# The first mixer's norm by another road: turned on VectorE and ScalarE between interleaved units, with the entrance norm's weights put in front of x and tile 0 fetched first

## The chip, the core and the metric

The kernel runs on one core of a Trainium2 chip. Its engines work side by side, each through its own list of instructions in order: TensorE (PE) multiplies matrices into PSUM, VectorE (DVE) and ScalarE (ACT) do elementwise work, GpSimd (POOL) does little here, and SyncE (SP) issues DMA transfers, which 16 DMA engines carry. They wait for each other by semaphores. The metric is device time in microseconds (us) from the kernel's start to its end; lower is better.

## The reference, cut to what matters

Two layers on x of 256 tokens by 1024 channels. The change touches the first half of layer 0, a gated short convolution:

```python
def rms_norm(x, g):
    y = x * lax.rsqrt(jnp.mean(x * x, axis=-1, keepdims=True) + EPS)
    return y * g

def short_conv_mixer(h, w_in, conv_w, w_out):
    b_gate, c_gate, hx = jnp.split(h @ w_in, 3, axis=-1)
    return (b_gate * causal_dwconv(c_gate * hx, conv_w)) @ w_out

x = x + short_conv_mixer(rms_norm(x, a_norm), a_w_in, a_conv, a_w_out)
x = x + conv_glu_ffn(rms_norm(x, f_norm[0]), ...)
# then shared K/V, attention, a second conv_glu_ffn, a last rms_norm
```

All is float32.

## The kernel before

x stands transposed in SBUF, channels on partitions, as 8 tiles k of [128 channels, 256 tokens]. Weights come in *units*: B units of 1 MB (128 x 2048) and S units of 0.5 MB (128 x 1024). To keep float32's accuracy with fast matmuls, each operand is split into a high and a low half: `hi(tag)` makes ACT write the high half of the next unit of that size (a rounding copy), `lo(tag)` makes DVE write the low half (raw minus high) of the next one; both may do a part, as in `hi("B", 0, 4)`, the first quarter. After the last part of a low half, the raw buffer is free and SP issues the load of the unit three further on. `hi` does nothing if the unit whose high buffer it would overwrite has not been given to TensorE yet. A product is three matmuls (`mm3`): high weight by high x, high weight by low x, low weight by high x.

The mixer has eight units of channels j. MC[j] (B) gives c_gate and hx, MB[j] (S) gives b_gate, MO[j] (S) is the row block of the output matrix. B units come in the order MC[0] to MC[7], then the FFN's; S units MB0, MB1, MB2, MB3, MO0, MO1, MB4, MO2, MB5, MO3 and so on. TensorE's order is MC0 and MB0 (in four quarters along k, as x and weights land), MC1, MB1, MC2, MB2, MC3, MB3, MO0, MO1, MC4, MB4, MO2, MC5 ...

The norm's weight is applied to x before the split (`scaled_hi`, `scaled_lo`), the per-token factor (the row rr, and its square in `rr[:, 1, :]`) after the matmuls: `mixer_a(j)` forms u = c * rr^2 * hx on DVE (two products), starts the convolution cv on ACT, does two taps and a product on DVE; `mixer_b(j)` multiplies by b_gate and splits the result z[j], high half on ACT and low half on DVE. So no unit can leave PSUM before rr is known, while units 0 to 2 are multiplied without it. In PSUM there are three `up` banks, four `acc` banks and one `misc`.

Here rr comes from `rstd_cols` and `rstd_rows`: TensorE sums the squares over partitions into columns (line 371), DVE takes the root, makes diagonal matrices dh and dl of it (lines 382, 383), and TensorE spreads them to all partitions by a matmul with ones (`each`, line 390). The FFN and attention norms use `sums`, `roots`, `spread` and `rows`: a transpose on DVE in 32 x 32 blocks, a reduction, three small ACT copies that bring four groups of 32 partitions together, a second reduction, the root (a first guess and three rounds of three instructions) on 32 partitions, three copies back, and a transpose that broadcasts.

At the start ten matmuls on `ones` (line 142) keep TensorE at work until data lands. `pk` holds all norm weights and convolution weights; its first 72 columns come over ACT's queue. `xh.again` and `xl.again` are copies of x tile 0 at another address; `up_step(..., again=True)` reads them instead of tile 0. The order of all this is written out by hand; no scheduler moves it.

Of the kernel before, what the change touches and what calls it, by code (L numbers as in the profile page):

```python
# [11 lines left out]
F32 = mybir.dt.float32  # L12
# [25 lines left out]
def f32(ap):  # L38
    return ap.bitcast(F32)
# [3 lines left out]
def yoco_kernel(ctx: ExitStack, tc: tile.TileContext, t: dict, out: bass.AP):  # L43
# [18 lines left out]
    class Unit:  # L62
# [12 lines left out]

        def load(self, part=0, parts=1):
# [3 lines left out]
            nc.sync.dma_start(self.raw[:, c], self.src[:, c])  # L80

# [55 lines left out]
    ones = const.tile([128, 128], F32, name="ones")  # L137
    G.memset(ones, 1.0)
    each = const.tile([128, 192], F32R, name="each")[:, 48:176]
    warm = psum.tile([128, 512], F32, name="misc", bufs=1)  # L140
    for _ in range(10):
        PE.matmul(warm[:, :128], ones, ones, start=True, stop=True)  # L142
# [21 lines left out]
    def par(c, k=0):  # L164
        return pk[:, c + k:c + k + 1]

# [66 lines left out]
    def acc_bank():  # L233
        return psum.tile([128, 2, S], F32, name="acc", bufs=4)
# [108 lines left out]

    def roots(sq):

        t = sq[0:32, 4, :]
        w = tmp.tile([128, 8], F32, name="nw")
        ms = t[:, 32:40]
        V.tensor_reduce(ms, t[:, 0:32].rearrange("p (a b) -> p b a", a=4), axis=mybir.AxisListType.X, op=OP.add)
# [17 lines left out]
    def rstd_cols(sq, meanwhile=None):

        ps = psum.tile([128, 512], F32, name="misc", bufs=1)
        for c in range(2):  # L370
            PE.matmul(ps[:, c:c + 1], sq[:, 2, c * 128:(c + 1) * 128], ones[:, 0:1],
                      start=(c == 0), stop=True, skip_group_check=True)
        w = tmp.tile([128, 8], F32, name="nw")
        ms, y, a = w[:, 0:2], w[:, 2:4], w[:, 4:6]
        V.tensor_scalar(ms, ps[:, 0:2], 1.0 / D, EPS, op0=OP.mult, op1=OP.add)
        rsqrt(ms, y, a)
        if meanwhile:
            meanwhile()
        dh, dl = (tmp.tile([128, 384 + 64], F32R, name="d" + x, tag="z" + x, bufs=4)[:, 16:16 + S] for x in "hl")
        for c in range(2):  # L380
            d = slice(c * 128, c * 128 + 128)
            V.tensor_scalar(dh[:, d], ident, y[:, c:c + 1], None, op0=OP.mult)
            V.scalar_tensor_tensor(dl[:, d], ident, y[:, c:c + 1], f32(dh[:, d]), op0=OP.mult, op1=OP.subtract)
        return y, (dh, dl)

    def rstd_rows(dg, scales=(1.0,), orders=(same,)):

        ps = psum.tile([128, 512], F32, name="misc", bufs=1)
        for n in range(2):
            PE.matmul(ps[:, :S], each, dg[n], start=(n == 0), stop=(n == 1), skip_group_check=True)  # L390
        r = act.tile([128, 2, S], F32, name="rr", bufs=1)
        for n, s in enumerate(scales):
            A.activation(r[:, n, :], orders[n](ps[:, :S]), AF.Copy, scale=s)
        return r

# [83 lines left out]
    rr = None  # L479

    def mixer_a(j, fill=None):

        w = [par(P_CONV, 3 * j + n) for n in range(3)]
        m = tmp.tile([128, 2, S], F32, name="u", bufs=2)
        V.tensor_mul(m[:, 1, :], mc[j][:, 0, :], rr[:, 1, :])
        V.tensor_mul(m[:, 0, :], mc[j][:, 1, :], m[:, 1, :])
        o = tmp.tile([128, 2, S], F32, name="cv", bufs=2)
        A.activation(o[:, 0, :], m[:, 0, :], AF.Identity, scale=w[2])
        hi("B")
        if fill:  # L490
            lo(fill)
        tap(o[:, 0, :], m[:, 0, :], w[1], 1)
        tap(o[:, 0, :], m[:, 0, :], w[0], 2)
        V.tensor_mul(o[:, 1, :], o[:, 0, :], rr[:, 0, :])
        return o[:, 1, :]

    def mixer_b(j, o, fill=None):
        hid = tmp.tile([128, S], F32, name="hid", tag="sc", bufs=4)
        V.tensor_mul(hid, mb[j][:, 0, :], o)
        z[j], zh, zl = split_act(hid, S)  # L500
        zh()
        if fill:
            lo(fill)
        zl()

    mc[1] = acc_bank()
    up_step(MC[1], mc[1], xh, xl, 2, range(1, 8), first=1)
    MC[1].used = False

    def quarter(q):  # L510
        hi("B", q, 4)
        lo("B", q, 4)

    _, dg = rstd_cols(sq, lambda: quarter(0))
    for q in range(1, 4):
        quarter(q)
    hi("S")
    hi("B")
    up_step(MC[1], mc[1], xh, xl, 2, (0,), first=1, again=True)
    MC[1].used = True  # L520
    mb[1] = acc_bank()
    up_step(MB[1], mb[1], xh, xl, 1, (*range(1, 7), 0, 7), first=1)
    mc[2] = up_bank()
    up_step(MC[2], mc[2], xh, xl, 2, range(0, 2))
    rr = rstd_rows(dg)
    A.activation(rr[:, 1, :], rr[:, 0, :], AF.Square)
    lo("S")
    up_step(MC[2], mc[2], xh, xl, 2, range(2, 8))
    mb[2] = psum.tile([128, 512], F32, name="misc", bufs=1).rearrange("p (a s) -> p a s", s=S)
    up_step(MB[2], mb[2], xh, xl, 1)  # L530
    for i in range(2):
        o = mixer_a(i, "B")
        hi("S")
        mixer_b(i, o, "S")
    hi("S")
    mc[3] = up_bank()
    up_step(MC[3], mc[3], xh, xl, 2, (1, 2, 3, 4, 5, 6, 0, 7), first=1, again=True)
    mixer_b(2, mixer_a(2, "S"))
# [34 lines left out]
    def ffn(layer, xh, xl, sq, bank=down_bank, between=None):  # L573
# [468 lines left out]
def _lay_out(i):  # L1042
# [41 lines left out]
```

## Time and profile before

| | before |
|---|---|
| runs shown | 564.45, 565.1 and 804.78 us, median 565.1 |
| profiled execution | 564.47 us |
| its span, first to last instruction | 562.7 us |
| TensorE busy | 556.1 us (99%) |
| DVE busy | 473.5 us (84%) |
| ACT busy | 343.7 us (61%) |
| read from HBM | 106.65 MB, 191 GB/s over the span |

In the rows of the profile below, a row in order of time gives the start in us, the time that it took in us (of several merged instructions: from the first's start to the last's end), the engine, the line, the operation, output<-inputs by the program's names, the shapes, how many (x), and in brackets how long the engine was idle before and what ended that. Rows with one duration as min/median/max are groups of equal instructions, in ns. Matmuls are pipelined: one is listed with 0.28 us but the next starts 0.11 us after it.

### The profile page before, as it was taken

How to read it: one execution, taken by the hardware profiler on the slowest of the kernel's cores; microseconds unless marked ns; L12 is line 12 of the kernel's file. 1: busy time of each engine (PE TensorE's matmuls, PEld its weight loads, DVE VectorE, ACT ScalarE, POOL GpSimd, SP SyncE). 2: the span in 40 equal slices, each digit the busy share in tenths (PEclk: the TensorE clock that was granted, in tenths of full speed). 3: DMA queues.
4: the chain of work that ended last, by engine and by line, in shares of the span. 5: the costliest groups of instructions: out<-in, count | busy, mean ns of one | idle time of the engine just before them, and what ended most of it. 6: DMA issues, size and time to landing. Idle time of an engine off the chain costs nothing.

```text
span 562.7 us, 11827 instructions
## 1 busy us (share of the span) xinstructions
PE 556.1 (99%) x4890; PEld 552.4 (98%) x4890; DVE 473.5 (84%) x827; ACT 343.7 (61%) x541; POOL 9.6 (2%) x29
## 2 busy tenths in 40 slices
PE   9999999999999999999999999999999999999996
PEld 9999999999999999999999999999999999999995
DVE  6998869998877787787997999859999888889875
ACT  7765437756654565465767777657676456546444
POOL 0400000000000000000000000000000000000001
PEclk9999999999999999999999999999999999999998
DMA  8986583447446545645354566552656654563211
GB/s 293 389 303 226 191 295 119 167 155 263 174 181 225 194 160 209 225 171 204 112 193 158 201 211 216 193 220 86 246 194 225 225 195 162 206 223 114 76 39 75
DMA packets 24181, 108.48 MB, mean 193 GB/s; under 512 B 2736, under 2 KB 5440, under 8 KB 16192
## 3 DMA queue, kind: packets, MB, share of 16 engines
q1 hardware_dynamic: 23840, 107.43, 53.7%
q8 instruction: 38, 0.62, 0.4%
q10 hardware_dynamic: 288, 0.30, 0.2%
q14 instruction: 15, 0.12, 0.1%
HBM read 106.65 MB, written 1.07 MB: 191 GB/s over the span
## 4 chain that ended last, share of the span: by engine, by line
PE 98%; issue 0%; ACT 0%; POOL 0%; DVE 0%; POOLq 0%
PE up L169 20%; PE up L171 20%; PE up L170 19%; PE acc L169 7%; PE acc L171 7%; PE acc L170 7%; PE acc L200 3%; PE acc L202 3%; PE acc L203 3%; PE up L442 1%; PE up L817 1%; PE acc L687 1%; PE acc L690 1%; PE acc L689 1%; PE misc L142 1%; PE acc L742 1%
## 5 line engine op out<-in xcount | busy, mean ns | idle before, releaser
L169 PE MATMUL up<-xh,hiB 128*128 128x256 f32 x928 | 256.5, 276 | 0.0
L171 PE MATMUL up<-xh,loB 128*128 128x256 f32 x928 | 256.2, 276 | 0.0
L170 PE MATMUL up<-xl,hiB 128*128 128x256 f32 x928 | 256.2, 276 | 0.0
L169 PEld LDWEIGHTS up<-xh,hiB 128*128 128x128 f32 x928 | 174.2, 188 | 0.5 <-issue 0.3
L170 PEld LDWEIGHTS up<-xl,hiB 128*128 128x128 f32 x928 | 174.2, 188 | 0.0
L171 PEld LDWEIGHTS up<-xh,loB 128*128 128x128 f32 x928 | 174.2, 188 | 0.0
L97 DVE TENSOR_TENSOR loB<-rawB,hiB 128x2048 fp32r<-128x2048 f32 (+3 forms) x80 | 148.2, 1856 | 3.7 <-ACT hiB L91 3.6
L91 ACT ACTIVATE hiB<-rawB 128x2048 fp32r<-128x2048 f32 (+2 forms) x75 | 123.8, 1657 | 11.7 <-PE up L170 4.3
L588 ACT ACTIVATE cv<-u,pk 128x256 f32<-128x256 f32 x88 | 48.2, 595 | 69.6 <-DVE u L581 69.4
L97 DVE TENSOR_TENSOR loS<-rawS,hiS 128x1024 fp32r<-128x1024 f32 (+2 forms) x73 | 83.5, 1146 | 6.8 <-ACT hiS L91 6.8
L426 DVE SCALAR_TENSOR_TENSOR cv<-u,pk,cv 128x255 f32<-128x255 f32 x192 | 81.3, 478 | 2.7 <-ACT cv L588 1.7
L91 ACT ACTIVATE hiS<-rawS 128x1024 fp32r<-128x1024 f32 (+2 forms) x73 | 72.0, 987 | 9.4 <-PE acc L170 5.2
L171 PE MATMUL acc<-sh,loS 128*128 128x256 f32 x240 | 66.2, 276 | 0.0
L169 PE MATMUL acc<-sh,hiS 128*128 128x256 f32 x240 | 66.2, 276 | 0.0
L170 PE MATMUL acc<-sl,hiS 128*128 128x256 f32 x240 | 66.2, 276 | 0.0
L581 DVE TENSOR_TENSOR u<-up,rr 128x512 f32<-128x512 f32 x44 | 30.3, 688 | 42.6 <-PE up L171 42.2
L423 ACT ACTIVATE sh<-hid 128x256 fp32r<-128x256 f32 x52 | 21.7, 417 | 58.4 <-DVE hid L605 53.7
L169 PEld LDWEIGHTS acc<-sh,hiS 128*128 128x128 f32 x240 | 45.1, 188 | 0.0
L170 PEld LDWEIGHTS acc<-sl,hiS 128*128 128x128 f32 x240 | 45.1, 188 | 0.0
L171 PEld LDWEIGHTS acc<-sh,loS 128*128 128x128 f32 x240 | 45.0, 188 | 0.0
L200 PE MATMUL acc<-hiS,sh 128*128 128x256 f32 x154 | 42.5, 276 | 0.0
L202 PE MATMUL acc<-loS,sh 128*128 128x256 f32 x154 | 42.5, 276 | 0.0
(209 smaller groups left out, 791.1 us busy)
## 6 DMA issues: line engine op xcount, KB each, us to landing
rawB<-w_up SPq DMA_DIRECT2D x44, 1024.0 KB, 4.7
rawS<-w_dn SPq DMA_DIRECT2D x44, 512.0 KB, 3.4
rawB<-w_qk SPq DMA_DIRECT2D x8, 1024.0 KB, 4.7
rawB<-w_mc SPq DMA_DIRECT2D x6, 1024.0 KB, 8.0
rawS<-w_mo SPq DMA_DIRECT2D x8, 512.0 KB, 5.4
rawB<-w_v SPq DMA_DIRECT2D x4, 1024.0 KB, 4.8
rawS<-w_o SPq DMA_DIRECT2D x8, 512.0 KB, 4.4
rawS<-w_mb SPq DMA_DIRECT2D x7, 512.0 KB, 5.8
```

Of the source, the lines that this page charges most:

```text
L91: A.activation(self.hi[:, c], self.raw[:, c], AF.Copy)
L97: V.tensor_sub(self.lo[:, c], self.raw[:, c], f32(self.hi[:, c]))
L169: PE.matmul(o, wh, xh, start=start, stop=False, skip_group_check=True)
L170: PE.matmul(o, wh, xl, start=False, stop=False, skip_group_check=True)
L171: PE.matmul(o, wl, xh, start=False, stop=stop, skip_group_check=True)
L200: PE.matmul(o, hh[:, tok], u.hi[:, f], start=(first and (apart or d.start == 0)), stop=False, skip_group_check=True)
L202: PE.matmul(o, hh[:, tok], u.lo[:, f], start=False, stop=False, skip_group_check=True)
L203: PE.matmul(o, hl[:, tok], u.hi[:, f], start=False, stop=last, skip_group_check=True)
L423: return (h, lw), lambda: A.activation(h, src, AF.Copy), lambda: V.tensor_sub(lw, src, f32(h))
L426: V.scalar_tensor_tensor(o[:, back:], u[:, :S - back], w, o[:, back:], op0=OP.mult, op1=OP.add)
L581: V.tensor_mul(u, ub[j], rr[:, 0:1, :].to_broadcast([128, 2, S]))
L588: A.activation(o[:, half, :], u[:, half, :], AF.Identity, scale=cw[half][2], bias=par(P_FCB, c0 + half * FJ))
```

## The change

Four things are changed together. (1) At the entrance, the eight weights of the first norm and 56 columns of padding stand in front of x in one array; tile 0 with them is the first transfer, tile 1 the second, MC[0]'s first eighth is issued by ACT, and tile 0 and its weights are split before tile 1 is touched. DVE instead of POOL writes `ones`, and seven warm-up matmuls run instead of ten. `pk` comes in one transfer, later. (2) rr comes by `sums`, `roots`, `spread`, `rows`, with quarters of MC[2]'s splits between their steps; `rstd_cols` and `rstd_rows` go, and the copy of xl's tile 0 moves from DVE to ACT. (3) `mixer_a` and `mixer_b` are cut into `mixer_u`, `mixer_t`, `mixer_z` and a separate low half, and for units 0 to 3 these are interleaved with each other and with the splits in a new order. MC[1] is multiplied in one go, tile 0 as copy and seventh. (4) The FFN's third unit in layer 0 reads a copy of tile 0, which ACT makes after the first.

```diff
     ones = const.tile([128, 128], F32, name="ones")
-    G.memset(ones, 1.0)
-    each = const.tile([128, 192], F32R, name="each")[:, 48:176]
+    V.memset(ones, 1.0)
+    spare = const.tile([128, 192], F32, name="each")
-    for _ in range(10):
+    for _ in range(7):
         PE.matmul(warm[:, :128], ones, ones, start=True, stop=True)
+    MC[0].load(0, 8, nc.scalar)
-    A.activation(each, ones, AF.Copy)
-    xT = act.tile([128, KT, S], F32, name="xres", bufs=1)
-    nc.scalar.dma_start(pk[:, :P_FCW], t["pk"][:, :P_FCW])
-    for q in range(4):
-        nc.sync.dma_start(xT[:, 2 * q:2 * q + 2, :], t["xT"][:, 2 * q:2 * q + 2, :])
+    xg = act.tile([128, 64 + KT * S], F32, name="xres", bufs=1)
+    xT = xg[:, 64:].rearrange("p (k s) -> p k s", s=S)
+    for a, b in ((0, 64 + S), (64 + S, 64 + 2 * S)):
+        nc.sync.dma_start(xg[:, a:b], t["xT"][:, a:b])
+    MC[0].load(1, 8)
+    MB[0].load(0, 4)
+    for q in range(1, 4):
+        a = 64 + 2 * q * S
+        nc.sync.dma_start(xg[:, a:a + 2 * S], t["xT"][:, a:a + 2 * S])
         MC[0].load(q, 4)
         MB[0].load(q, 4)
...
-    nc.sync.dma_start(pk[:, P_FCW:], t["pk"][:, P_FCW:])
+    nc.sync.dma_start(pk, t["pk"])
...
         if q == 0:
             scaled_hi(xT, P_AN, (0,), xh)
+            scaled_lo(xT, P_AN, (0,), xh, xl)
+            hi("B", 0, 8)
+            lo("B", 0, 8)
             V.tensor_scalar(xh[:, 1, :], xT[:, 1, :], par(P_AN, 1), None, op0=OP.mult)
+            scaled_lo(xT, P_AN, (1,), xh, xl)
+            hi("B", 1, 8)
+            lo("B", 1, 8)
...
+    A.activation(xh.again, f32(xh[:, 0, :]), AF.Copy)
+    A.activation(xl.again, f32(xl[:, 0, :]), AF.Copy)
     sum_squares(sq, 1)
-    tile_0_again(xh, xl)
     hi("S")
...
+    mc[1] = acc_bank()
+    up_step(MC[1], mc[1], xh, xl, 2, (*range(1, 7), 0, 7), first=1, again=True)
+
+    hi("B", 0, 4)
+    lo("S")
+    sums(sq)
+    for q in range(1, 4):
+        hi("B", q, 4)
+    lo("B", 0, 4)
+    y = roots(sq, lambda: lo("B", 1, 4))
+    spread(y)
+    hi("S")
+    lo("B", 2, 4)
+    rr = root_rows()
+    rows(y, rr[:, 0, :])
+    lo("B", 3, 4)
+    hi("B")
+    mb[1] = acc_bank()
+    up_step(MB[1], mb[1], xh, xl, 1)
+    mc[2] = up_bank()
+    A.activation(rr[:, 1, :], rr[:, 0, :], AF.Square)
+    lo("S")
+    up_step(MC[2], mc[2], xh, xl, 2)
...
+    up_step(MB[2], mb[2], xh, xl, 1)
+    mixer_u(0)
+    hi("B")
+    lo("B")
+    mixer_t(0)
+    hi("S")
+    zl = mixer_z(0)
+    mixer_u(1)
+    zl()
+    lo("S")
+    hi("S")
+    mixer_t(1)
+    zl = mixer_z(1)
+    mixer_u(2)
+    zl()
     hi("S")
     lo("S")
+    lo("S")
+    hi("B")
+    lo("B")
+    mc[3] = up_bank()
+    up_step(MC[3], mc[3], xh, xl, 2, (1, 2, 3, 4, 5, 6, 0, 7), first=1, again=True)
+    mixer_t(2)
+    zl = mixer_z(2)
+    mb[3] = up_bank()
+    up_step(MB[3], mb[3], xh, xl, 1)
+    mixer_u(3)
     hi("S")
     hi("B")
+    zl()
     lo("S")
+    mixer_t(3)
+    mixer_z(3)()
+    lo("B")
     acc = [acc_bank() for _ in range(4)]
     for i in range(2):
         down_step(MO[i], acc, z[i], first=(i == 0))
         hi("S")
         lo("S")
...
+            again = i == 2 and not layer
+            up_step(up[i], ub[i], xh, xl, 2, (*range(1, 7), 0, 7) if again else range(8), first=int(again), again=again)
             if i == 0:
                 sums(sq)
+                if not layer:
+                    A.activation(xh.again, f32(xh[:, 0, :]), AF.Copy)
+                    A.activation(xl.again, f32(xl[:, 0, :]), AF.Copy)
```

The old order of units 0 to 3, in short: u, cv, high MC, low MC, taps, high S, product, high half, low S, low half, one unit after the other.

More of the change, by code (lines that the diff above doesn't have):

```diff
@@ L74, in __init__, with load @@
             mine.append(self)
-        def load(self, part=0, parts=1):
+        def load(self, part=0, parts=1, eng=nc.sync):
             if self.raw is None:
@@ L79, in load @@
             c = slice(part * self.n // parts, (part + 1) * self.n // parts)
-            nc.sync.dma_start(self.raw[:, c], self.src[:, c])
+            eng.dma_start(self.raw[:, c], self.src[:, c])
         def buffer(self, name):
@@ L164, in par @@
     def par(c, k=0):
-        return pk[:, c + k:c + k + 1]
+        return (xg if c == P_AN else pk)[:, c + k:c + k + 1]
     def mm3(o, wh, wl, xh, xl, start, stop):
@@ L321, in all_squares, with rsqrt @@
         sum_squares(sq, 1, order)
-    def rsqrt(ms, y, a, eng=V):
+    def rsqrt(ms, y, a, mid=None, eng=V):
         eng.tensor_scalar(y.bitcast(I32), ms.bitcast(I32), -0.5, float(0x5F3759DF), op0=OP.mult, op1=OP.add)
-        for _ in range(3):
+        for n in range(3):
+            if n == 2 and mid:
+                mid()
             eng.tensor_mul(a, y, y)
@@ L364, in root_rows @@
         return act.tile([128, 2, S], F32, name="rr", bufs=1)
[L367 to L394, printed above, removed]
     ext_d = dram.tile([NH, 384], F32, name="ext_d")
@@ L458, in yoco_kernel @@
                 lo("B", k, 8)
-        else:
+        elif q:
             hi("B", q, 4)
@@ L474, in yoco_kernel, with mixer_u @@
             sum_squares(sq, 0)
+    A.activation(xh.again, f32(xh[:, 0, :]), AF.Copy)
+    A.activation(xl.again, f32(xl[:, 0, :]), AF.Copy)
     sum_squares(sq, 1)
-    tile_0_again(xh, xl)
+    hi("S")
+    rr = None
+    uu, oo = {}, {}
+    def mixer_u(j):
+        m = uu[j] = tmp.tile([128, 2, S], F32, name="u", bufs=2)
+        V.tensor_mul(m[:, 1, :], mc[j][:, 0, :], rr[:, 1, :])
+        V.tensor_mul(m[:, 0, :], mc[j][:, 1, :], m[:, 1, :])
+        o = oo[j] = tmp.tile([128, 2, S], F32, name="cv", bufs=2)
+        A.activation(o[:, 0, :], m[:, 0, :], AF.Identity, scale=par(P_CONV, 3 * j + 2))
@@ new lines, in mixer_t, with mixer_z, mixer_a @@
+    def mixer_t(j):
+        m, o = uu[j], oo[j]
+        tap(o[:, 0, :], m[:, 0, :], par(P_CONV, 3 * j + 1), 1)
+        tap(o[:, 0, :], m[:, 0, :], par(P_CONV, 3 * j), 2)
+        V.tensor_mul(o[:, 1, :], o[:, 0, :], rr[:, 0, :])
+    def mixer_z(j):
+        hid = tmp.tile([128, S], F32, name="hid", tag="sc", bufs=4)
+        V.tensor_mul(hid, mb[j][:, 0, :], oo[j][:, 1, :])
+        z[j], zh, zl = split_act(hid, S)
+        zh()
+        return zl
+    def mixer_a(j, fill):
+        mixer_u(j)
+        hi("B")
+        lo(fill)
+        mixer_t(j)
@@ new lines, in mixer_b @@
+    def mixer_b(j, fill):
+        zl = mixer_z(j)
+        lo(fill)
+        zl()
[17 more added lines that the diff above has]
+    up_step(MB[1], mb[1], xh, xl, 1)
@@ L477, in yoco_kernel @@
+    mc[2] = up_bank()
+    A.activation(rr[:, 1, :], rr[:, 0, :], AF.Square)
+    lo("S")
+    up_step(MC[2], mc[2], xh, xl, 2)
+    mb[2] = psum.tile([128, 512], F32, name="misc", bufs=1).rearrange("p (a s) -> p a s", s=S)
+    up_step(MB[2], mb[2], xh, xl, 1)
[8 more added lines that the diff above has]
+    lo("S")
+    hi("S")
+    mixer_t(1)
+    zl = mixer_z(1)
+    mixer_u(2)
+    zl()
     hi("S")
     lo("S")
-    rr = None
@@ L481, in mixer_a @@
[L481 to L516, printed above, removed]
+    lo("S")
@@ L517, in yoco_kernel @@
+    hi("B")
+    lo("B")
[6 more added lines that the diff above has]
+    mixer_u(3)
     hi("S")
     hi("B")
[L519 to L524, printed above, removed]
@@ L525, in yoco_kernel @@
-    rr = rstd_rows(dg)
-    A.activation(rr[:, 1, :], rr[:, 0, :], AF.Square)
-    lo("S")
[L528 to L538, printed above, removed]
@@ L555, in yoco_kernel @@
         hi("S")
-        mixer_b(j, o, "B" if j < KT - 1 else "S")
+        mixer_b(j, "B" if j < KT - 1 else "S")
         if j < KT - 1:
@@ L1047, in _lay_out @@
     r = {}
-    r["xT"] = c(a["x"][0].T.reshape(KT, 128, S).transpose(1, 0, 2))
+    r["xT"] = c(np.concatenate([cols(a["a_norm"][0]), np.zeros((128, 64 - KT), np.float32),
+                                a["x"][0].T.reshape(KT, 128, S).transpose(1, 0, 2).reshape(128, -1)], 1))
     win = kpc(a["a_w_in"][0]).reshape(KT, 128, 3, KT, 128)
```

17 lines of the change are left out of this document (6 added, 11 removed).

## The prediction

> **What bounds the kernel now.** I read the page's first part, the chain of work that ended last, then the busy time by stretch of time, and last the order of time of single engines between 0 and 56 us, the only part that the change reorders.
>
> ```profile
> span 562.7 us, 11827 instructions
> PE 556.1 (99%) x4890; PEld 552.4 (98%) x4890; DVE 473.5 (84%) x827; ACT 343.7 (61%) x541; POOL 9.6 (2%) x29
> ...
> PE 98%; issue 0%; ACT 0%; POOL 0%; DVE 0%; POOLq 0%
> ...
> 5.20:6.50 1.30, 1.30 (x9) 1.30 (x7) 0.98 (x3) 0.31 (x1) 0.00 (x0) 1.00 0.96 321
> ...
> 24.50:39.40 14.90, 14.90 (x134) 14.90 (x133) 14.55 (x22) 9.53 (x12) 2.90 (x5) 1.00 0.87 306
> 39.40:55.80 16.40, 16.40 (x147) 16.40 (x146) 14.72 (x25) 8.89 (x11) 0.00 (x0) 1.00 0.70 238
> ...
> 60.00:80.00 20.00, 20.00 (x179) 20.00 (x178) 16.95 (x21) 9.27 (x10) 0.00 (x0) 1.00 0.76 260
> ```
>
> TensorE is 98% of the chain and has no hole in any stretch. So only three things can change the time: matmuls fewer or more, the start of the stream, and new holes in it. In these rows stand the length, then busy time of PE, its weight loads, VectorE (DVE), ScalarE (ACT) and POOL, the granted clock, the DMA share and GB/s. DVE has 14.55 of 14.90 us in the mixer's first units: there it is nearly as tight as TensorE, so a delay on DVE soon becomes a hole.
>
> The entrance, in order of time:
>
> ```profile
> 0.99 4.64 PE L142 MATMUL misc<-ones 128*128 128x128 f32 x20 [0.99 <-POOL ones L138]
> ...
> 3.75 0.51 ACT L283 ACTIVATE xh<-xres,pk 128x256 fp32r<-128x256 f32 x1 [1.32 <-DMA pk<-pk]
> ...
> 5.29 0.77 PE L442 MATMUL up<-xh,hiB 128*128 128x256 f32 x2
> ...
> 6.73 0.91 ACT L283 ACTIVATE xh<-xres,pk 128x256 fp32r<-128x256 f32 x2 [1.22 <-DMA xres<-xT]
> ...
> 8.08 0.43 PE L442 MATMUL up<-xh,hiB 128*128 128x256 f32 x2
> ...
> 9.27 0.62 ACT L91 ACTIVATE hiB<-rawB 128x512 fp32r<-128x512 f32 x1
> ...
> 10.18 0.39 PE L442 MATMUL up<-xh,hiB 128*128 128x256 f32 x2
> ...
> 12.01 0.64 ACT L91 ACTIVATE hiB<-rawB 128x512 fp32r<-128x512 f32 x1 [0.16 <-DMA rawB<-w_mc]
> ...
> 15.97 0.68 DVE L97 TENSOR_TENSOR loB<-rawB,hiB 128x512 fp32r<-128x512 f32 x1
> ```
>
> The real stream starts at 5.29, right behind the warm-up matmuls. But the second quarter of x lands only at 6.73, its first matmul follows at 8.08, and ScalarE (ACT) waits for weights once more at 12.01. The entrance is paced by transfers.
>
> **The change part by part.** *Entrance.* Tile 0 and the norm's weights come in one small first transfer, and three warm-up matmuls go: at 4.64/10 = 0.46 us each, the warm-up ends near 4.1 instead of 5.3. The first pieces are half as large and land sooner than 3.75, so I put the first real matmul near 4.15, 1.1 us sooner. That lead does not last. Ahead of the second quarter stand the same bytes as before (x, two weight quarters; 36 KB of packed parameters go, 32 KB ahead of x come), and the sync queue issues four transfers before it instead of three. Its matmuls can start no sooner than about 7.5 to 8.1, and the third quarter's no sooner than the split at 9.27 + 0.62 and a handover, 9.95 against 10.18. Of 1.1 us some 0.2 stays; bounds are 0 and 1.1.
>
> The Trainium skill ("DMA: Bandwidth & Descriptors", section "Issuing engines are not separate DMA queues") says that transfers issued by different engines share the same 16 DMA engines and interleave, which speaks against issuing the first weight piece from ACT: by it x and the weights share what there is, as I took them. Were the queues apart, the lead of 1.1 us could last. That 0.96 of the DMA engines' time is busy at 5.2 to 6.5 agrees with the rule.
>
> *The norm.* Removed from TensorE are the sum over partitions and the spreading of the row:
>
> ```profile
> 19.02 0.50 PE L371 MATMUL misc<-ones,sq 128*128 128x1 f32 x4
> ...
> 19.38 0.37 PE L169 MATMUL acc<-xh,hiB 128*128 128x256 f32 x1
> ...
> 19.58 0.28 PE L170 MATMUL acc<-xl,hiB 128*128 128x256 f32 x1
> ...
> 20.05 0.27 PE L171 MATMUL acc<-xh,loB 128*128 128x256 f32 x1
> ...
> 24.26 0.28 PE L390 MATMUL misc<-dh,each 128*128 128x256 f32 x1
> ...
> 24.48 0.28 PE L169 MATMUL up<-xh,hiB 128*128 128x256 f32 x1
> ```
>
> That is 19.38 - 19.02 = 0.36, plus 0.09 (the next matmul follows after 0.20 instead of 0.11), plus 24.48 - 24.26 = 0.22: **0.67 us**. With the entrance, TensorE alone would gain 0.2 + 0.67 = 0.9 us.
>
> The new norm has the form that the FFN of this kernel already uses, so its pieces have rows:
>
> ```profile
> L339 DVE STREAM_TRANSPOSE sq<-sq x3: 445/445/447, 99.0 to 383.4; 128x256 f32<-128x256 f32 x3
> ...
> L340 DVE TENSOR_REDUCE sq<-sq x3: 419/419/421, 99.4 to 383.9; 128x8 f32<-128x256 f32 x3
> ...
> L342 ACT ACTIVATE sq<-sq x9: 206/208/211, 99.9 to 384.8; 32x8 f32<-32x8 f32 x9
> ...
> L349 DVE TENSOR_REDUCE sq<-sq x3: 196/196/199, 100.9 to 385.3; 32x8 f32<-32x32 f32 x3
> ...
> L361 DVE STREAM_TRANSPOSE rr<-nw x3: 425/425/425, 104.3 to 388.7; 128x256 f32<-128x256 f32 x3
> ...
> 18.36 0.28 DVE L279 CAST xl<-xl 128x256 fp32r<-128x256 f32 x1
> ...
> 23.24 0.35 DVE L383 SCALAR_TENSOR_TENSOR dl<-ident,nw,dh 128x128 fp32r<-128x128 f32 x1
> ```
>
> DVE gains 0.45 + 0.42 + 0.20 + 0.43 = 1.5 us and loses the four diagonal products (22.34 to their end at 23.59, 1.2 us) and the copy of tile 0 (0.28, now on ACT): no difference in work. What changes is who waits for whom, and it has to be walked.
>
> *The walk.* In the trace both engines run their instructions in the program's order, so I list them and give each its duration, the pitch at which it follows its neighbour, and its waits. Walking the old order in this way meets the old trace within 0.1 us up to 50 us. The prices:
>
> ```profile
> 20.83 1.04 ACT L91 ACTIVATE hiS<-rawS 128x1024 fp32r<-128x1024 f32 x1
> ...
> 23.09 1.92 ACT L91 ACTIVATE hiB<-rawB 128x2048 fp32r<-128x2048 f32 x1 [1.22 <-PE acc L171]
> ...
> 25.32 0.42 ACT L526 ACTIVATE rr<-rr 128x256 f32<-128x256 f32 x1
> ...
> 27.36 0.51 ACT L488 ACTIVATE cv<-u,pk 128x256 f32<-128x256 f32 x1 [1.63 <-DVE u L486]
> ...
> 26.45 0.42 DVE L485 TENSOR_TENSOR u<-up,rr 128x256 f32<-128x256 f32 x1
> ...
> 27.24 2.28 DVE L97 TENSOR_TENSOR loB<-rawB,hiB 128x2048 fp32r<-128x2048 f32 x1
> ...
> 43.42 0.43 DVE L423 TENSOR_TENSOR sl<-hid,sh 128x256 fp32r<-128x256 f32 x1 [0.48 <-ACT sh L423]
> ...
> 46.76 1.00 DVE L426 SCALAR_TENSOR_TENSOR cv<-u,pk,cv 128x255 f32<-128x255 f32 x2
> ...
> 50.18 1.23 DVE L97 TENSOR_TENSOR loS<-rawS,hiS 128x1024 fp32r<-128x1024 f32 x1
> ...
> 53.32 0.28 PE L171 MATMUL acc<-sh,loS 128*128 128x256 f32 x1
> ...
> 55.81 0.28 PE L169 MATMUL up<-xh,hiB 128*128 128x256 f32 x1
> ```
>
> I start at the split of MC[1]'s last quarter on DVE (15.97), whose place the transfers set (shift 0, bounds -0.2 and +0.3). Sums of squares to 18.46, low half of MB[1] to 19.6, transpose and reduction to 20.4, three ACT copies to 21.1, the root with a quarter's low half inside it to 23.9, three ACT copies to 24.6. Now ACT splits MB[2] (to 25.65) and all of MC[3] (to 27.5) **before** it squares rr: rr is whole at 27.8, where it was at 25.74. DVE is through with MB[2]'s low half at 26.9 and stands idle about 0.9 us. u(0) takes 27.8 to 28.7, MC[3]'s low half 28.6 to 30.9. On from there, without holes: unit 0's taps and product to 32.75, u(1), MB[3] low to 35.0, unit 1 to 36.9, u(2), MO[0] low to 39.1, MO[1] low to 40.4, MC[4] low to 42.6, unit 2's taps and product to 44.5, u(3) to 45.3.
>
> Then the second wait. MB[4]'s high half stands on ACT behind cv(3), so it runs 45.7 to 46.8; DVE, done with unit 2's low half at 45.6, waits 1.2 us. MB[4] low ends 48.0, unit 3's product 49.9. Its low half follows its high half on ACT with nothing between: 0.5 us more, done 50.8. MC[5]'s low half, formerly ahead of unit 3's taps, runs to 53.0, and **MO[2]'s low half ends at 54.1**. Before, it started at 50.18. The three waits, 0.9 + 1.2 + 0.5, are the 2.7 us by which it starts later.
>
> TensorE meanwhile: the pitch is (55.81 - 24.48)/276 matmuls = 0.1135 us, and MC[1] starts two quarters (36 matmuls) after 9.95, at 14.05, instead of 14.26. MC[3] would take its first low product at 30.6; MC[3]'s low half is at TensorE at 30.9 + 0.17, a hole of 0.4. MO[0] loses 0.1. It reaches MO[2]'s first low product at 52.9, and this can run at 54.1 + 0.17 = 54.3: **a hole of 1.4 us**. MO[2] ends at 56.8, where MC[5] begins; it began at 55.81. From there DVE has holes of its own (16.95 busy of 20.00 after 60) and nothing else is late. The balance at MC[5] is -0.2 - 0.67 + 0.4 + 0.1 + 1.4 = **+1.0 us**. A consequence: MO[2]'s wait does not ask when TensorE arrived, so what the entrance saves or loses there, up to 1.4 us, doesn't count.
>
> *The rest.* The two copies of tile 0 in the FFN (0.4 us each on ACT) stand before a whole unit's split that has over 5 us to spare; third unit's tile 0 costs 6 matmuls at 0.12 instead of 0.113, 0.04 us. The larger parameter transfer is 40 KB, 0.1 us at the 306 GB/s above, needed 7 us after it lands. The extra 64 columns ahead of x cost nothing if addresses don't matter.
>
> **The sum.** The profiled execution took 564.47 us (span 562.7), so 565.5; the median shown is 565.1, which gives 566.1. I take 565.7 between the two.
>
> **The rivals.** *The gain is kept.* If ACT's splits fall earlier than I walk them (0.9 and 1.2 us of the waits are gone as soon as the splits of MC[3] and MB[4] are not in the way), the MO[2] hole closes and 0.9 us stays: 563.6, or 564.2 on the median. For it speaks that ACT is busy only 9.53 of 14.90 us; against it that order, not load, makes it late.
>
> *Addresses.* x grows by 256 bytes a partition, so xh and xl lie elsewhere against the weights. Tile 0's copy shows the price: 19.58 to 20.05 is four matmuls at 0.1175, 4 to 5 ns over the usual. If all 928 x 3 matmuls of the page's up groups ran so, 2784 x 4.5 ns = 12.5 us: 578, slower by 2.2%. It decides if the relative place of xh and weights, not the copy, makes the pitch. Against it: both buffers of xh and all three weight slots run at the same count in every stretch.
>
> *The entrance turns late.* TensorE's matmuls run at 0.21 us up to about 6.5 (a pair takes 0.77 at 5.29 and 0.39 at 10.18), though the granted clock stands at 1.00 for 5.2 to 6.5. With a hole in the early stream the slow spell could last through the second quarter: 18 x 0.1 = 1.8 us, 0.4 beyond what MO[2]'s hole hides, so 566.1 to 566.5. The same result comes from transfers 0.5 us late, which shift DVE's walk whole. The Trainium skill ("TensorE: Matmul & The Clock Gate", section "Part 1: The HAM clock gate") has a free-running window of some 3.4 us in which the array must be busy before the clock is released; the 5.5 us from 0.99 to 6.5 fit one to two windows. By that rule seven warm-up matmuls, followed at once by real ones, lose nothing.
>
> *It does not do what it says:* the entrance gains nothing at all. By the walk this changes the end by nothing.
>
> **Chances.** The walk's holes, 0.60 (565.1 to 566.4); gain kept, 0.26 (563.6 to 564.5); entrance late, 0.12 (566.1 to 566.9); addresses, 0.02. Two in a hundred, 11 us, is about what a measurement of this kernel tells from no change; no case but the addresses reaches it. Range 563.6 to 566.8; faster 0.01, same 0.97, slower 0.02.
>
> **What would show it.** First real matmul near 4.2 but the third quarter's near 10; rr squared at 27.4 to 27.8 behind a 2048-column split; a DVE wait of about 1.2 us before MB[4]'s low half; MO[2]'s first low matmul at 54.3 behind a hole of 1.4 us. I am wrong if TensorE stays without holes between 30 and 57 us, or if the matmul pitch anywhere leaves 0.113.

## The result, and the profile after

The changed kernel takes **567.5 us** (median of six runs, 567.0 to 569.7) against 565.1 for the kernel before: ratio 1.0052, 95% interval 1.0042 to 1.0061. That is slower, by less than the 2% that one measurement tells from no change. The forecast was 565.7, at most 566.8. Medians and ratios here and below leave out the executions near 575 us that some kernels had, and one of 804.78 us of the kernel before. The profiled execution has a span of 565.8 us, 3.1 more than before. From the page of the changed kernel, span, busy times and shares of the chain:

```profile
span 565.8 us, 11811 instructions
...
PE 555.6 (98%) x4878; PEld 550.5 (97%) x4878; DVE 474.5 (84%) x827; ACT 346.0 (61%) x548; POOL 8.1 (1%) x28
...
PE 88%; DVE 5%; ACT 2%; DMA 2%; issue 1%; SPq 0%; POOL 0%; POOLq 0%; DVEq 0%; ACTq 0%
```

TensorE works 0.5 us less, yet the span is longer: the chain has left TensorE for 12% of its length. Where, the order of time on TensorE shows (changed kernel):

```profile
4.76 0.50 PE L419 MATMUL up<-xh,hiB 128*128 128x256 f32 x2 [0.35 <-ACT hiB L91]
...
11.71 0.51 PE L419 MATMUL up<-xh,hiB 128*128 128x256 f32 x2 [1.05 <-ACT hiB L91]
...
15.91 0.28 PE L174 MATMUL acc<-xh,hiB 128*128 128x256 f32 x1
...
32.39 0.28 PE L175 MATMUL up<-xl,hiB 128*128 128x256 f32 x1
32.78 0.39 PE L176 MATMUL up<-xh,loB 128*128 128x256 f32 x1
...
33.12 0.28 PE L175 MATMUL up<-xl,hiB 128*128 128x256 f32 x1
...
37.62 0.28 PE L174 MATMUL up<-xh,hiB 128*128 128x256 f32 x1
...
54.75 0.28 PE L175 MATMUL acc<-sl,hiS 128*128 128x256 f32 x1
56.18 0.39 PE L176 MATMUL acc<-sh,loS 128*128 128x256 f32 x1 [1.16 <-DVE loS L97]
...
58.80 0.28 PE L174 MATMUL up<-xh,hiB 128*128 128x256 f32 x1
```

The row at 15.91 is the first matmul of MC[1] (14.26 before), the last one that of MC[5] (55.81 before). The first real matmul is earlier than before, 4.76 against 5.29, but the third quarter's is later, 11.71 against 10.18. Two holes follow: 0.4 us at MC[3]'s first low product and 1.4 us at MO[2]'s. The balance at MC[5] is +1.65 (MC[1]) - 0.67 (the norm) + 0.4 + 1.4 + 0.2 (MC[3]) = +2.98, measured +2.99. The 0.2 is a slower pace: from 33.12 to 37.62 are 38 matmuls, 118.4 ns each instead of 113.3. The splits on ScalarE in the same kernel:

```profile
3.89 0.51 ACT L288 ACTIVATE xh<-xres 128x256 fp32r<-128x256 f32 x1 [1.22 <-DMA xres<-xT]
...
7.06 0.91 ACT L288 ACTIVATE xh<-xres 128x256 fp32r<-128x256 f32 x2 [0.68 <-DMA xres<-xT]
...
9.87 0.91 ACT L288 ACTIVATE xh<-xres 128x256 fp32r<-128x256 f32 x2 [0.98 <-DMA xres<-xT]
...
11.02 0.63 ACT L91 ACTIVATE hiB<-rawB 128x512 fp32r<-128x512 f32 x1 [0.24 <-DMA rawB<-w_mc]
...
27.41 1.90 ACT L91 ACTIVATE hiB<-rawB 128x2048 fp32r<-128x2048 f32 x1
29.22 0.40 ACT L522 ACTIVATE rr<-rr 128x256 f32<-128x256 f32 x1
```

And VectorE:

```profile
17.76 0.69 DVE L97 TENSOR_TENSOR loB<-rawB,hiB 128x512 fp32r<-128x512 f32 x1
...
29.65 0.42 DVE L469 TENSOR_TENSOR u<-up,rr 128x256 f32<-128x256 f32 x1 [0.88 <-ACT rr L522]
...
48.82 1.22 DVE L97 TENSOR_TENSOR loS<-rawS,hiS 128x1024 fp32r<-128x1024 f32 x1 [1.26 <-ACT hiS L91]
...
52.36 0.43 DVE L400 TENSOR_TENSOR sl<-hid,sh 128x256 fp32r<-128x256 f32 x1 [0.48 <-ACT sh L400]
...
54.91 1.22 DVE L97 TENSOR_TENSOR loS<-rawS,hiS 128x1024 fp32r<-128x1024 f32 x1
```

The second and third quarters of x are split at 7.06 and 9.87 (6.73 and 8.47 before). The first piece, though smaller, is split at 3.89, no sooner than before (3.75). MC[1]'s last low quarter, where the walk began, stands at 17.76 instead of 15.97. Everything behind it is where the walk put it, 1.8 to 2.0 us later. Two rows of each kernel's transfers in the first 14 us (packets and MB moved; then KB per transfer and median us from issue to landing), and one of its busy time from 7.5 to 9.5 us (the last two numbers are the DMA engines' busy share and GB/s), show what came of the transfers. Before:

```profile
DMA packets 2537, 4.07 MB, mean 291 GB/s; under 512 B 402, under 2 KB 914, under 8 KB 2535
...
xres<-xT SPq DMA_DIRECT2D x4, 256.0 KB, 4.7
...
7.50:9.50 2.00, 2.00 (x20) 2.00 (x18) 2.00 (x7) 2.00 (x7) 0.00 (x0) 1.00 1.02 369
```

After:

```profile
DMA packets 2512, 3.58 MB, mean 256 GB/s; under 512 B 271, under 2 KB 1295, under 8 KB 2512
...
xres<-xT SPq DMA_DIRECT2D x3, 256.0 KB, 5.8
...
7.50:9.50 2.00, 1.41 (x13) 1.22 (x12) 1.89 (x5) 1.39 (x5) 0.00 (x0) 1.00 0.92 221
```

In the same time half a megabyte less was moved, and a quarter of x took 1.0 us longer to land (the 4.7 before counts the first quarter too; the three that match those after have 4.8). From 7.5 to 9.5 us, where the third quarter was due, the DMA engines show as busy for 0.92 of the time and yet moved 221 GB/s instead of 369.

### The profile page after: what moved, and what is told of

It reads as the page before. It is cut to its first block, busy times and chain, and to the rows that moved or that the text cites. A ratio compares the mean times of both kernels' runs of the same rounds, so it can differ in the third digit from the quotient of the medians.

```text
span 565.8 us, 11811 instructions
## 1 busy us (share of the span) xinstructions
PE 555.6 (98%) x4878; PEld 550.5 (97%) x4878; DVE 474.5 (84%) x827; ACT 346.0 (61%) x548; POOL 8.1 (1%) x28
## 4 chain that ended last, share of the span: by engine, by line
PE 88%; DVE 5%; ACT 2%; DMA 2%; issue 1%; SPq 0%; POOL 0%; POOLq 0%; DVEq 0%; ACTq 0%
PE up L174 18%; PE up L176 18%; PE up L175 18%; PE acc L176 6%; PE acc L174 6%; PE acc L175 6%; PE acc L208 3%; PE acc L207 3%; PE acc L205 3%; DMA xres<-xT 1%; DVE loB L97 1%; DVE loS L97 1%; PE up L837 1%; PE acc L710 1%; PE acc L707 1%
```

## The experiments

Every time is a median of 5 to 12 runs, beside runs of the kernel before on the same chip (medians 564.8 to 564.9).

**The two halves apart.** e1 has the new entrance with the old norm and order, e2 the old entrance with the new norm and order.

> The new entrance with the old norm and the old order of the units. Theory T (the transfers of the new entrance land up to 2 us later and push everything behind them): the last low quarter of MC[1] on VectorE starts near 17.8 us instead of 15.97 as in the changed kernel, MC[1]'s matmuls near 15.9, no new hole in the mixer, and the time is that of the kernel before plus about 1.7 us: some 566.2 us, ratio 1.003. Rival M (the new norm and order cost all of the 3.1 us, and the late landings are bad luck or follow from them): the transfers land as in the kernel before and the time is within 0.4 us of it.

> The old entrance with the new norm and the new order of the units. Theory T with the walk of the prediction: a hole of 0.4 us before MC[3]'s first low product and of 1.3 to 1.4 us before MO[2]'s, MC[5] starts at 56.8 instead of 55.81, the time is that of the kernel before plus 0.8 to 1.1 us, ratio 1.0015 to 1.002. Rival M: plus 2.5 to 3.1 us, ratio 1.005.

e1 took 565.9 (ratio 1.0017, 1.0009 to 1.0026). MC[1] starts at 15.82, 1.56 later than before, and nothing is late after it: MC[5] starts at 57.38, 1.57 later. So the new entrance alone costs instead of gaining, 1.0 us by the medians and 1.6 in the profiled executions (1.7 was expected). e2 fell into two groups, three runs at 565.8 to 566.3 and three at 567.9 to 568.3 (1.0041, 1.0026 to 1.0056). The lower group, 1.3 us above before, fits the walk's holes (0.8 to 1.1 was expected); the profiles of e8 and e11 below, which have the same order, start MC[5] at 57.33 and 57.19, 1.5 and 1.4 later than before. The profile of e2 is one of the upper group. TensorE in e2:

```profile
53.47 0.28 PE L169 MATMUL acc<-sl,hiS 128*128 128x256 f32 x1
54.41 0.39 PE L170 MATMUL acc<-sh,loS 128*128 128x256 f32 x1 [0.67 <-DVE loS L97]
...
57.12 0.28 PE L168 MATMUL up<-xh,hiB 128*128 128x256 f32 x1
```

With the old entrance the low half of MO[2] was walked to reach TensorE at 54.3: it did at 54.41. MC[5] begins at 57.12 (walk: 56.8). The other 2 us of the upper group come later, and the busy time by stretch shows them (length; busy us and count of PE, then of the other engines; granted clock, DMA share, GB/s):

```profile
54.70:112.90 58.20, 58.20 (x496) 58.20 (x496) 49.28 (x81) 34.33 (x49) 0.00 (x0) 1.00 0.58 205
...
115.00:173.00 58.00, 58.00 (x514) 58.00 (x513) 48.82 (x75) 35.39 (x48) 0.00 (x0) 1.00 0.54 190
```

The same matmuls, without holes and at a granted clock of 1.00, take 58.2/494 = 117.8 ns in one stretch and 58.0/512 = 113.3 ns in the next (each count holds two that began before its stretch). More on this below.

**The waits that the order makes.** e4 is e2 with three waits taken away by order alone; e7 does the same in the changed kernel.

```diff
+    A.activation(rr[:, 1, :], rr[:, 0, :], AF.Square)
     hi("B")                      # all of MC[3]
...
-    A.activation(rr[:, 1, :], rr[:, 0, :], AF.Square)
...
+    hi("S")                      # MB[4]
     mixer_u(3)
-    hi("S")
...
-    mixer_z(3)()
-    lo("B")
+    zl = mixer_z(3)
+    lo("B")                      # MC[5]
+    zl()
```

> The old entrance and the new norm, but with the three waits of the walk taken out by order alone: rr is squared before MC[3] is split, MB[4]'s high half goes ahead of unit 3's u, and MC[5]'s low half stands between unit 3's high and low half. Theory T with the walk: no hole before MC[3] and MO[2]; what is left is the 0.67 us of matmuls that the old norm took, so 0.4 to 0.8 us faster than the kernel before, ratio 0.9985 to 0.9993. If the holes come from something else (slower VectorE work as such), the time stays at the level of the old entrance with the new order unmended.

> The changed kernel with its own entrance, and the three waits taken out by order as before. If the holes before MC[3] and MO[2] come from the order alone (the walk), both go and with them the slow pitch in MC[3]: 0.4 + 0.2 + 1.4 = 2.0 us off 567.5, so 565.3 to 565.9. If the late entrance makes them, at least one of more than 0.5 us stays and the time is above 566.3.

e4 took **564.26** (564.0 to 564.7; ratio 0.9990, 0.9981 to 0.9998) and e7 565.5 (1.0009, 1.0000 to 1.0018). TensorE in e4 at MO[2]'s first low product:

```profile
53.06 0.28 PE L169 MATMUL acc<-sl,hiS 128*128 128x256 f32 x1
53.17 0.28 PE L170 MATMUL acc<-sh,loS 128*128 128x256 f32 x1
...
55.66 0.28 PE L168 MATMUL up<-xh,hiB 128*128 128x256 f32 x1
```

The hole is gone, with the same instructions in another order. So the order makes the holes and the norm without TensorE is a gain: e4 is the fastest kernel here whose runs all agree, 0.6 us below before, as expected from the 0.67 removed. Between e7 and e4 lie 1.2 us, and the two kernels differ in the entrance alone.

**What in the entrance is late.** The changed kernel differs from before in who issues (ScalarE one transfer), in x's rows (8448 bytes instead of 8192) and in its first pieces. e3 has the sync queue issue MC[0]'s first eighth. e5 gives x its old rows, with the norm's weights in a transfer of their own on ScalarE's queue, ahead of MC[0]'s first eighth. e6 keeps the new rows and takes large first pieces again. e9 is the kernel before with the new rows alone, e10 the kernel before with the small pieces alone:

```diff
-    for q in range(4):
+    nc.sync.dma_start(xT[:, 0, :], t["xT"][:, 0, :])
+    MC[0].load(0, 8)
+    nc.sync.dma_start(xT[:, 1, :], t["xT"][:, 1, :])
+    MC[0].load(1, 8)
+    MB[0].load(0, 4)
+    for q in range(1, 4):
```

> The changed kernel, but MC[0]'s first eighth is issued by the sync engine behind tile 0, not by ScalarE. If the second issuing queue is what slows the early transfers (theory Q), the second and third quarters of x land as early as in the kernel before (6.7 and 8.4 us) and the time falls by 1 us or more, to 566.5 or less. If the number and size of the early pieces do it (theory S), landings and time stay within 0.4 us of the changed kernel (567.5).

> The changed kernel with x again in rows of 8192 bytes in memory and the norm's weights as a small transfer of their own on ScalarE's queue; pieces, order and place in SBUF stay. If the odd row pitch (8448 bytes) of x slows the early transfers (theory P), x's third quarter lands near 8.4 us instead of 9.85 and the time falls by 1 us or more, to 566.5 or less. If the number and size of the pieces do it (theory S), it stays within 0.4 us of the changed kernel's 567.5.

> The changed kernel with the old cut of the first transfers: x's first quarter (with the norm's weights ahead of it) in one, MC[0]'s first quarter in one, all on the sync queue; the row pitch of 8448 bytes stays. Theory S: x's third quarter lands near 8.4 us, and the time falls by 1 us or more, to 566.5 or less. Theory P: landings as late as in the changed kernel (9.85), time within 0.4 us of 567.5.

> The kernel before with one change: x lies in memory in rows of 8448 bytes, 256 bytes of padding ahead of each, instead of 8192; transfers, sizes and all the rest stay. Theory P (the odd pitch slows the transfers of x and all behind them): MC[1]'s matmuls start 0.5 us or more later than 14.26 and the time rises by 0.5 to 1.2 us, ratio 1.001 to 1.002. Theory S: no change, within 0.3 us.

> The kernel before with one change: the first quarters of x and of MC[0] go in two transfers each (tile 0, first eighth, tile 1, second eighth); pitch and all the rest stay. Theory S (more and smaller pieces slow the early transfers): plus 0.5 to 1.0 us. Theory P: within 0.3 us of the kernel before.

The start of MC[1]'s last low quarter on VectorE is a measure of the entrance, since what stands ahead of it is paced by transfers:

| kernel | entrance | last low quarter, us | time minus before, us |
|---|---|---|---|
| before, e2, e4, e8, e11 | old | 15.97, 16.00, 16.41, 16.30, 16.15 | |
| e9 | old, new rows | 16.29 | +0.1 |
| e5, e12 | new pieces, old rows | 16.55, 16.81 | |
| e6 | old pieces, new rows | 16.86 | +2.0 |
| after, e1, e7 | new | 17.76, 17.60, 17.40 | |
| e3 | new, no issue by ScalarE | 17.44 | +2.9 |
| e10 | old, new pieces | 17.77 | +1.5 |

One and the same entrance scatters by 0.44 us between profiles, and the new one lies 1.4 us above the old, without overlap. e3 (567.8; 1.0063, 1.0049 to 1.0077) shows that ScalarE's issue is not the cause: the third quarter of x is split at 9.88 against 9.87, although it was issued 0.40 later (4.47 against 4.07). The Trainium skill ("DMA: Bandwidth & Descriptors", section "Issuing engines are not separate DMA queues") says that transfers issued by different engines run on the same 16 DMA engines and interleave, with which these times agree. e9 (564.9; 1.0006, 0.9997 to 1.0014) shows that the new rows alone cost nothing. e10 (566.35; 1.0027, 1.0017 to 1.0037) shows that the small pieces alone cost 1.5 us, as much as the whole new entrance (1.0 in e1, 1.2 between e7 and e4; 0.5 to 1.0 was expected). Its transfers in the first 14 us:

```profile
DMA packets 2614, 3.52 MB, mean 251 GB/s; under 512 B 411, under 2 KB 1435, under 8 KB 2614
...
xres<-xT SPq DMA_DIRECT2D x3, 256.0 KB, 5.8
```

These are close to the changed kernel's two numbers. But e5 (568.3; 1.0062, 1.0049 to 1.0075) and e6 (566.9; 1.0047, 1.0033 to 1.0060) meet neither theory's range and don't fit a sum of parts: small pieces with the old rows are late by 0.4 to 0.6, large pieces with the new rows by 0.7, though the new rows alone are late by 0.1. So taking one part back out of the changed kernel does not single out its cause. Both times seem to hold the slower matmuls of the last part of this section too (e5: two runs near 566.5, four at 568.2 to 569.2).

**Size or number.** The small pieces have two sides: they are small, and there are two more of them. e14 is the kernel before with its own pieces and two transfers of 256 bytes which nothing reads; e17 issues those two from ScalarE. e13 is e10 with half of the small pieces issued by ScalarE. e15 and e16 start from e4: MB[0]'s quarters issued by ScalarE, and MB[0] fetched as two halves.

```diff
     MC[0].load(q, 4)
+    if q == 0:                   # e14; e17: ahead of the loop, by nc.scalar
+        for i in range(2):
+            nc.sync.dma_start(spare[i:i + 1, :], t["pk"][i:i + 1, :64])
```

> The kernel before, with tile 0 and tile 1 of x and the two eighths of MC[0] in transfers of their own, as in e10, but tile 1 and the second eighth issued by ScalarE's queue: so the sync queue issues the third quarter of x as early as before (near 3.5 us, 4.48 in e10). Theory I (what makes the small pieces dear is the time of the two further issues on the sync queue, 0.47 us each): the third quarter of x is split near 8.5 us, VectorE's last low quarter of MC[1] starts near 16.0, and the time is within 0.3 us of before (564.8 to 565.2). Theory S (the size itself makes the transfers slow, whoever issues them): split near 10.3, low quarter near 17.7, and 566.0 to 566.6.

> The kernel before with its own pieces, and two transfers of 256 bytes each, which nothing reads, issued by the sync queue in the first round, ahead of MB[0]'s first quarter: the third quarter of x is issued near 4.48 us as in e10, and the bytes are those of before. Theory I: landing as late as in e10, split of the third quarter at 9.5 to 10.3 us, and 565.8 to 566.4. Theory S: split near 8.5 and 564.8 to 565.2.

> e4 with MB[0]'s four quarters issued by ScalarE's queue, so that the sync queue issues two transfers a round instead of three and is 0.47 us earlier with each round. Theory I: the third quarter of x is split up to 0.9 us earlier than in e4, MC[1] starts 0.5 to 0.9 us earlier, and the time is 563.4 to 563.8, the fastest of all. Theory S, or if the bytes set the pace: as e4, 564.0 to 564.6.

> e4 with MB[0] fetched in two halves of 256 KB, with the first and the third quarter of the other weights, instead of four quarters: two transfers fewer on the sync queue, the same bytes ahead of the third quarter of x, 128 KB more ahead of the second. If each transfer on the sync queue costs 0.5 us or more as in e10 and e14 (theory I), the third quarter of x is split 0.4 to 0.8 us earlier than in the kernels with the old entrance (8.5 to 9.1 us), MC[1] starts near 13.6 to 14.0, and the time is 563.4 to 564.0, the fastest. If the bytes alone count, the second quarter comes 0.3 us later and the time is 564.2 to 564.8.

> The kernel before with e14's two transfers of 256 bytes issued by ScalarE's queue, behind its packed parameters: the sync queue issues the third quarter of x near 3.5 us as before. Theory I (the later issue on the sync queue is what e14 paid for): last low quarter of MC[1] at 15.9 to 16.4 us and 564.7 to 565.2. If the transfers themselves hold something up (a DMA engine, or one of the eight that are in flight at most), 17.0 to 17.8 and 565.6 to 566.4, as in e14.

| | time, us | ratio, interval | last low quarter | MB moved in 14 us |
|---|---|---|---|---|
| e14 | 566.1 | 1.0019, 1.0011 to 1.0028 | 17.77 | 3.59 |
| e17 | 566.5 | 1.0026, 1.0017 to 1.0035 | 18.22 | 3.42 |
| e13 | 567.3 | 1.0047, 1.0033 to 1.0061 | 18.58 | 3.12 |
| e15 | 566.1 | 1.0021, 1.0012 to 1.0030 | 17.83 | 3.39 |
| e16 | 564.0 (7 of 12 runs) | 0.9988, 0.9978 to 0.9998 | 16.64 | 4.25 |

**Theory S falls with e14**: half a kilobyte in two transfers costs about as much as the divided pieces (1.2 us beside 1.5, with overlapping intervals and the same last low quarter, 17.77). Theory I's cause, two times 0.47 us on the sync queue, **falls with e13, e15 and e17**: there the sync queue has no issue more, or fewer, and still its transfers go out late. In e13 the third quarter of x did come earlier than in e10 (landed at 8.74 against 10.32; 8.37 before), and the transfers behind it later than ever. The reason is seen best in e15, in the order of time of the sync queue's issues and then of ScalarE:

```profile
2.10 0.43 SPq L80 DMA_DIRECT2D rawB<-w_mc  x1
2.58 0.43 SPq L149 DMA_DIRECT2D xres<-xT  x1
6.75 0.33 SPq L80 DMA_DIRECT2D rawB<-w_mc  x1
```

```profile
0.98 0.38 ACTq L147 DMA_DIRECT2D pk<-pk  x1
1.39 0.93 ACTq L80 DMA_DIRECT2D rawS<-w_mb  x2
...
4.00 1.11 ACTq L80 DMA_DIRECT2D rawS<-w_mb  x2
5.15 0.51 ACT L282 ACTIVATE xh<-xres,pk 128x256 fp32r<-128x256 f32 x1 [2.92 <-DMA rawB<-w_mc]
```

Five transfers on the one queue (0.74, 1.17, 1.64 and the two above) and three on the other are out by 2.6 us; the ninth goes only at 4.00, when the first has landed (3.98 in the trace), and ScalarE's first split of x, queued behind its issues, runs at 5.15 (3.83 in e4). The sync queue's own waits, first in e15 and then in e17 (us in total, times, longest):

```profile
SPq L80 <- DMA xres<-xT: 3.7, 1, 3.7
```

```profile
SPq L153 <- DMA rawB<-w_mc: 0.8, 1, 0.8
```

**This program has at most eight transfers in flight over both queues**; each later one takes the place of one that has landed, and waits for it. In e17 the tiny transfers take two of the places, and the third quarter of x is issued at 4.76 for that reason, not at 3.53. So a transfer costs a place until it has landed, whatever it carries, and time on its queue, 0.47 us here (about 0.3 for the 256 bytes in e14). In the changed kernel the third quarter of x has become the ninth transfer: it is issued at 4.07 (0.47 later by the queue, 0.07 by its place) and lands at 9.85, 1.5 later. In e10 it is issued 0.95 later and lands 1.95 later. The later issue is thus at most a third to a half of the lateness, and even this share is not shown: e3 issues the third quarter later than the changed kernel and has it as early, and e5 and e12 issue it at 4.05 and 4.00, as the changed kernel does, and have it at 8.79. The rest, transfers that take a microsecond longer while busy DMA engines move less, is **open**: e5, with as many small ones, moved 3.92 MB in 14 us, and no row of the traces tells why it should differ from e10. Nor do fewer transfers show a gain: e16, with two fewer, is at 564.0 beside e4's 564.26 (ratios 0.9988 and 0.9990), and in its profile MC[1] starts at 14.78, as in e4 (14.77), not at 13.6 to 14.0. Its upper five runs belong to the next part.

**The slower matmuls.** Theory R: after a small hole TensorE may go on at 117.8 ns a matmul instead of 113.3, until it next reads a copy of tile 0. In e2 it ended at the FFN's copy (113.08), in the changed kernel at MC[3]'s own copy (37.7). e8 is e2 without the FFN's copy, e11 also reads a copy in MC[5]. e12 is e5 with the three waits removed.

```diff
-            again = i == 2 and not layer
+            again = False                                    # e8, e11
...                                                            # for unit 5:
+        up_step(MC[5], mc[5], xh, xl, 2, (*range(1, 7), 0, 7), first=1, again=True)   # e11
```

> The old entrance with the new order of the mixer, unmended, and the FFN's third unit reading tile 0 itself instead of its copy. In the profile of the old entrance with the new order, matmuls followed each other at 117.8 ns from a hole at 39.5 us on up to the unit that reads the copy, at 113 us, and at 113.3 after it; the times fell into two groups, near 566.0 and near 568.2. Theory R (a hole can set a slower pace that lasts until matmuls read a copy of tile 0): the first group stays near 566.0 and the other lies far higher, as the pace lasts past 113 us up to the next copy near 290: about 4.5 ns x 1560 matmuls = 7 us more, near 575. Rival E (the pace ends by itself, or with the FFN's first units): the two groups stay where they were, at most 568.5.

> The old entrance with the new order of the mixer, unmended; the copy of tile 0 is read in MC[5], right behind the unit in which the hole falls, and not in the FFN. Theory R (a hole can set a slower pace that lasts until matmuls read a copy of tile 0): one group of times, 565.6 to 566.5, no runs near 568 or 575. Rival E (the pace ends for another reason): groups near 566 and near 568 or 575 as before.

> The changed kernel with x in rows of 8192 bytes, the norm's weights as their own transfer, and the three waits taken out by order. Theory P: beside the same kernel with the odd pitch (565.6) it gains 0.7 to 1.2 us, 564.4 to 564.9. Theory S: within 0.4 us of 565.6.

e8: nine runs at 565.5 to 566.7 (1.0022, 1.0013 to 1.0031) and three at 574.4 to 575.0. e11: eleven runs in one group, 565.5 to 566.2 (1.0018, 1.0009 to 1.0027), none near 568 or 575. So far the times are as R had them. e8's own profile (565.95) is not:

```profile
20.00:50.00 30.00, 30.00 (x257) 30.00 (x256) 26.38 (x53) 18.61 (x26) 5.83 (x17) 1.00 0.75 268
60.00:90.00 30.00, 30.00 (x267) 30.00 (x267) 24.55 (x32) 14.11 (x16) 0.00 (x0) 1.00 0.72 253
```

With 257 matmuls in 30 us and then 267, the slow pace ran there from 10 us on, past the copies that MC[1] and MC[3] read, and ended at the hole before MO[2]'s low half (54.7), where no copy is read. The profiles of e5 and e6 end it at the same hole. It cost this execution next to nothing, as it only made the hole smaller (MC[5] starts 0.14 later than in e11). e12 took 565.3 (1.0007, 0.9998 to 1.0016), within 0.4 of e7's 565.5, so it bears out its theory S: x's rows are not what the entrance pays. Its profiled execution is the one at 574.8, and it too **contradicts R**. Its busy time by stretch:

```profile
60.00:80.00 20.00, 20.00 (x172) 20.00 (x171) 15.99 (x20) 8.21 (x9) 0.00 (x0) 1.00 0.74 260
...
260.00:280.00 20.00, 20.00 (x173) 20.00 (x171) 15.01 (x26) 9.20 (x15) 0.57 (x2) 1.00 0.53 191
...
380.00:400.00 20.00, 20.00 (x179) 20.00 (x178) 15.38 (x35) 11.78 (x23) 0.00 (x0) 1.00 0.27 90
```

172 or 173 matmuls in 20 us up to 290 us, past three copies of tile 0, then 179. e16's profiled execution (574.6) is another such one: 172 from 60 to 80 and from 260 to 280 us, 179 from 380 on; 5 of its 12 runs lie at 574.4 to 575.3, of the kernel before 3 of 120 at 574.4 to 574.9 (these were not profiled). The slow pace and its price are shown, 4.5 ns a matmul, 2.2 us for 496 of them and some 10 us up to 290. What starts it and what ends it is not: a copy can end it (e2, e11) and need not (e8, e12), and a hole stood at its start in e2 and at its end in e5, e6 and e8, but MO[2]'s hole in e2 did not end it.

## Why the prediction was wrong, point by point

- **The failed step is the entrance's term.** It said that "some 0.2 stays" of 1.1 us, with bounds 0 and 1.1, and gave VectorE's start a "shift 0, bounds -0.2 and +0.3". Measured: TensorE's MC[1] +1.65, VectorE's start +1.79 (the new entrance's three profiles lie 1.4 above the old one's five in the mean). By the prediction's own walk VectorE's start is what counts, and from 0 to +1.79 is all of the 1.8 us by which the forecast was low. I counted the bytes ahead of the second quarter, which were the same, and wrote down the fourth issue, but priced neither it nor the place in flight that it takes. What the runs showed in its place: two further transfers in the first round, even of 256 bytes, cost 1.2 to 1.7 us (e10, e14, e17). Why the transfers behind them then land a microsecond later than their issue explains, and what in the changed kernel, which has only one more ahead of the third quarter, does it, stays open.
- The case was among the rivals, as "transfers 0.5 us late, which shift DVE's walk whole", at 0.12. The mechanism was right, the size a third of what came. The consequence that the text drew, that MO[2]'s wait hides what the entrance loses, holds for TensorE's arrival alone and was of no use here: the transfers set VectorE's start as well, and so MO[2]'s low half moved with them (54.91; walked 52.9).
- The first real matmul, 4.76 against "near 4.15": the first pieces did not "land sooner than 3.75" (split at 3.89), so MC[0]'s first eighth was split late, and TensorE waited 0.35 us for it behind the warm-up matmuls.
- The norm's 0.67 us was right: e4's TensorE comes to MC[5] 0.15 earlier though it began MC[1] 0.5 later, which is 0.66.
- **The walk was right in every wait**: 0.9, 1.2 and 0.5 us were forecast, 0.88, 1.26 and 0.48 measured; rr squared stands behind MC[3]'s split of 2048 columns; the holes of 0.4 and 1.4 us are 0.4 and 1.4. MO[0]'s 0.1 did not show. That MO[2]'s hole kept its size was luck: TensorE and VectorE both came there about 2 us later than walked. e4 removes the holes by order alone. One sign of being wrong that the text gave did come: the pitch left 0.113, for 38 matmuls behind MC[3]'s hole (118.4 ns, 0.2 us), which the sum did not have.
- "The gain is kept" was the other likely rival, and it needed "the splits of MC[3] and MB[4]" out of the way: moved there in e4, they gave 564.26, where 563.6 or 564.2 was forecast.
- Addresses: the price of 4 to 5 ns a matmul was right, its condition wrong. It is no matter of x's rows (e9); it comes and goes within one kernel, between runs. The FFN's copy cost about 0.05 us (111.83 to 113.13 is eleven matmuls at 118 ns), 0.04 forecast.

## What to carry to other kernels

Before dividing a first transfer to have its first part sooner, count the transfers as well as the bytes: each costs an issue (0.3 to 0.47 us here) and a place among those in flight (eight here), and the ones behind may pay; then measure, as the price here (1.2 to 1.7 us for two) was larger than its parts explain. When an order is changed by hand, list both elementwise engines with their durations and look for what stands ahead of each result on its engine; such a walk met every wait here to 0.1 us, and the list of waits was also the list of what to move. A lead of one engine is worth nothing if the transfers behind it make the second engine start later.

## What was not expected of the hardware

- TensorE has a second steady pace: 128 x 256 matmuls at 117.8 ns instead of 113.3, with no hole and a granted clock of 1.00 in both. It can last from a few us to 280 us, and in some traces it began or ended right behind a hole, under 0.1 us long (e2 at 39.4 us, e5 at 31.6) or longer (e8 at 54.4).
- Two transfers of 256 bytes delayed a stream of 4 MB by 1.6 to 2.0 us (last low quarter 17.77 and 18.22 against 15.97 to 16.41, 16.2 in the mean).
- DMA engines that show as busy can move little: 221 GB/s at a busy share of 0.92 in the changed kernel, 369 at 1.02 before, from 7.5 to 9.5 us.
